# A hybrid encoder layer on one core: the queues planned with later landings and longer issues for the scan's loads

## The chip, the cores and the metric

The kernel runs on one core of one Trainium2 chip. The time is that of one execution in device microseconds. Before the change three runs took 1288.22, 1292.00 and 1293.46 us; their median is 1292.0.

The core's engines each run a queue of their own in order: TensorE (PE) for matmuls, with PEld for its weight loads, VectorE (DVE), ScalarE (ACT), GpSimd (POOL), and SyncE (SP), which here issues every transfer. An instruction that waits holds up all that stands behind it in its queue.

## The reference

One layer of an encoder, sequence 2048, width 1024, all in fp32. A normalised input is projected once; the columns go to two groups of heads, whose results are joined, projected and added to the input.

```python
h = rms_norm(x, norm_w)
dn_q, dn_k, dn_v, dn_z, dn_beta, dn_decay, sw_q, sw_k, sw_v, sw_z = split(h @ w_in)
# A: 4 heads of 128, gated delta rule, forward and backward
q, k, v = silu(depthwise_conv5(concat(dn_q, dn_k, dn_v)))
q, k = l2_norm(q) * 128 ** -0.5, l2_norm(k)
fwd = delta_rule(q, k, v, g[:, :, 0], beta[:, :, 0])
bwd = flip(delta_rule(flip(q, k, v, g[:, :, 1], beta[:, :, 1])))
dn = rms_norm(fwd + bwd, out_norm_w) * silu(dn_z)
# B: 8 query heads of 64, 2 key heads, |i - j| <= 128, QK-norm, rotary, a sink logit per head
sw = windowed_attention(sw_q, sw_k, sw_v) * silu(sw_z)
x = x + concat(dn, sw) @ w_out

def delta_rule(q, k, v, g, beta):       # per chunk: t_inv = (I + m)^-1, then a scan over chunks
    v_new = u - w @ state
    o = (q * exp(g)) @ state + a @ v_new
    state = state * exp(g_last) + k_dec.T @ v_new
```

## The kernel before

**Stages.** `phase_a` makes the projections in two halves of 1024 rows. A fp32 product is made of three matmuls, with weights and input split into a high and a low part (`wh`/`wl`, `xhi`/`xlo`): `pf_c` and `pf_z` are projections with the features on the partitions, `pq` with the rows there. Attention for 128 rows at a time runs between them (`s`, `pt`, `po`). The convolution is made on VectorE in `acc`. Results go to DRAM: `kq_d` and `v_d` per delta head, `zdn` and `zsw_d` for the gates, `mix_sw` for the attention.

`phase_b` does the delta rule, chunks of 128 rows, two directions (`d`), heads 0 to 3. `pre_front(h)` loads k and q (`kq`, 512 rows each, two buffers), transposes them (`tr`), makes their products (`gh`) and the decayed matrices `ma`, which go to DRAM as `m_d`. `pre_back(h)` inverts: it loads the diagonal 32x32 blocks of `m_d` into `L0` and `L` and unit matrices into `X` (from `eye`), solves them in 31 steps on VectorE (`tm`, `X`, lines L704 and L708), writes `X` to DRAM as `x_d`, reads it back in blocks as `xc` (two directions by four groups of chunks), spreads these to `ut` and `tt`, and joins the blocks with matmuls `pza`, `pra`, `pzb`, `prb`. `scan(h)` then goes over 16 steps in both directions; each step loads `at` (64 KB of `m_d`) and, from the second on, `kqc` (128 KB of `kq_d`), each with three buffers per direction:

```python
at = rp.tile([P, P], F32, tag=f"at{d}", name=f"at{nm}", bufs=3)
dma(at, m_d[d, c, : 2 * P * P].rearrange("(i a j) -> i a j", a=2, j=P)[:, 1])
kqc = rp.tile([P, 2, P], F32, tag=f"kqc{d}", name=f"kqc{nm}", bufs=3)
dma(kqc, kq_d[h][:, :, sc])
T.matmul(pk, kqc[:, 0], st[d], start=True, stop=True)
```

The matmul above (L785) is the first of a step, `po<-S,kqc` (L795) the last reader of `kqc`, and `po<-y,at` (L811) that of `at`. `post` norms and gates a head (`tro`, `zt`) and stores it in `mix_dn`.

The output projection has two halves. That of the attention (`pcs`, weights `woss`, inputs `mls`) has no part in the chain of the delta heads; its 16 chunks are put between the scans, and the partial sums go to DRAM as `part`. That of the delta heads (`pcd`, weights `wosd`, inputs `mld`, and `xrd` and `x2d`, the partial sum and the residual) ends the program.

**What sets the order.** The code does not. `set_order` takes all instructions and plans the five queues together: it gives each a price (`cost` for the time on its engine, SP's issues included; `landing` for the time from a transfer's issue until its reader may start), walks forward and backward with the prices, tries 120 random variations with a fixed seed, and keeps the plan that ends first by its own prices. The plan is then fixed as the order of each queue. So a price changes no instruction, only the order.

Of the kernel before, what the change touches and what calls it, by code (L numbers as in the profile page):

```python
# [892 lines left out]
def set_order(tc):  # L893
# [9 lines left out]
    n = len(insts)  # L903
    tiles = {x.name: x for x in tc.tiles}

    def aps(l):
        return [a.bass_ap for a in l if hasattr(a, "bass_ap")]

    def size(a):
        r = 1  # L910
        for _, c in list(a.ap)[1:]:
            r *= c
        return r
# [107 lines left out]
    def cost(i, eng):  # L1021
        o = aps(i.outs)
        m, ins = size(o[0]), aps(i.ins)
        if eng == "SP":
            dims = max(sum(c > 1 for _, c in list(a.ap)[1:]) for a in (o[0], ins[0]))
            return 450 if dims < 2 else 560
        off = 115 * (o[0].ap[0][0] > 0 and o[0].offset // o[0].ap[0][0] % P > 0)
        if eng == "PE":
            if i.is_transpose:
                return 110  # L1030
            if "float32r" in str(i.ins[0].dtype):
                return max(111, 0.4435 * m + 5.5)
            return 2 * max(m * 0.855, 112)
        scalars = sum(size(a) == 1 for a in ins)
        if eng == "Activation":
            psum = any("PSUM" in str(tiles[a.tensor.name].space) for a in ins if a.tensor.name in tiles)
            return 82 - 42 * psum + 0.865 * m + 92 * (scalars > 0) + 92 * (len(o) > 1) + off
        m = max([m] + [size(a) for a in ins])
        if eng == "DVE":
            if i.opcode == "Reciprocal":  # L1040
                return 62 + 6.2 * m
            if i.opcode == "TensorScalarPtr" and len(ins) - scalars < 2:
                return 58 + 0.6 * m
            return 68 + 1.04 * m + 60 * (scalars > 0) + 10 * (i.opcode == "ISA") + off
        if i.opcode == "TensorTensor":
            return 350 + 160 * m if m <= 16 else 140 + 2.165 * m
        return 250 + 0.8 * m + 0.4 * off

    def landing(i):
        o, a = aps(i.outs)[0], aps(i.ins)[0]  # L1050
        n = o.ap[0][1] * size(o) * 4
        if o.tensor.name in tiles and "DRAM" in str(tiles[o.tensor.name].space):
            return 1800 + n / (450 if sum(c > 1 for _, c in o.ap) < 3 else 190)
        run = min([c for t, c in list(a.ap) + list(o.ap) if t == 1] or [1])
        return 1900 + n / 190 + 1000 * any(t == 0 for t, _ in a.ap) + 1200 * (run < 64)

    total = len(succ)
    dur = [cost(i, e) for i, e in insts] + [0] * (total - n)
    eng = [e for _, e in insts] + [None] * (total - n)
    move, late = [0.0] * total, [0.0] * total  # L1060
    nxt, prv = [[] for _ in range(total)], [[] for _ in range(total)]
    for k in range(total):
        if eng[k] == "SP":
            a = aps(insts[k][0].outs)[0]
            move[k] = a.ap[0][1] * size(a) * 4 / 300
            late[k] = landing(insts[k][0])
        lag = LAG[eng[k]] + late[k] if k < n else 0
        if eng[k] == "Activation" and len(aps(insts[k][0].outs)) > 1:
            lag += 90
        for s in succ[k]:  # L1070
            if eng[s] == eng[k] != "SP":
                nxt[k].append((s, SAME[eng[k]] * ((k, s) in wrote)))
            else:
                nxt[k].append((s, lag))
        for s in started[k] if k < n else ():
            nxt[k].append((s, None))
        for s, d in nxt[k]:
            prv[s].append((k, d))
# [182 lines left out]
```

## Time and profile before

| | |
|---|---|
| median of three runs | 1292.0 us |
| execution that was profiled | 1291.88 us |
| its span, first to last instruction | 1290.1 us |
| mean granted TensorE clock | 0.989 |
| TensorE busy | 1220.2 us (95%) |
| VectorE busy | 939.1 us (73%) |
| ScalarE, GpSimd busy | 700.8 us, 486.3 us |
| moved by DMA | 218.01 MB, mean 169 GB/s |

Busy times are unions over the span. In rows of the timeline the first number is the start after the span's start in us, the second the duration; SPq rows are the issues of transfers, whose duration includes a wait at the head of the queue. In square brackets stands how long the engine was idle ahead of the row, and what ended that.

### The profile page before, as it was taken

How to read it: one execution, taken by the hardware profiler on the slowest of the kernel's cores; microseconds unless marked ns; L12 is line 12 of the kernel's file. 1: busy time of each engine (PE TensorE's matmuls, PEld its weight loads, DVE VectorE, ACT ScalarE, POOL GpSimd, SP SyncE). 2: the span in 40 equal slices, each digit the busy share in tenths (PEclk: the TensorE clock that was granted, in tenths of full speed). 3: DMA queues.
4: the chain of work that ended last, by engine and by line, in shares of the span. 5: the costliest groups of instructions: out<-in, count | busy, mean ns of one | idle time of the engine just before them, and what ended most of it. 6: DMA issues, size and time to landing. Idle time of an engine off the chain costs nothing.

```text
span 1290.1 us, 22274 instructions
## 1 busy us (share of the span) xinstructions
PE 1220.2 (95%) x7034; PEld 1043.6 (81%) x7034; DVE 939.1 (73%) x2346; ACT 700.8 (54%) x2057; POOL 486.3 (38%) x606
## 2 busy tenths in 40 slices
PE   4999999999999999999999999699999999998998
PEld 4998878888899987787778877587788788986776
DVE  4312477777888778799997878789779888766443
ACT  5322254435677777877755455476566655555211
POOL 1330214104667677886312313512422320213333
PEclk9999999999999999999999999799999999999999
DMA  8453244325542344421247567878868765378897
GB/s 259 129 144 104 82 145 146 119 86 173 162 123 81 113 117 135 137 88 67 74 146 265 177 175 240 221 190 256 236 158 255 248 160 159 100 230 272 250 309 227
DMA packets 238519, 218.01 MB, mean 169 GB/s; under 512 B 50624, under 2 KB 189632, under 8 KB 238400
## 3 DMA queue, kind: packets, MB, share of 16 engines
q1 hardware_dynamic: 238400, 216.58, 55.4%
q8 instruction: 56, 0.92, 0.3%
q14 instruction: 63, 0.52, 0.1%
HBM read 143.05 MB, written 73.47 MB: 168 GB/s over the span
## 4 chain that ended last, share of the span: by engine, by line
PE 75%; DMA 10%; DVE 6%; ACT 4%; issue 2%; SPq 2%; POOL 1%; DVEq 0%; ACTq 0%; POOLq 0%
PE pf_c L188 6%; PE pf_c L189 6%; PE pf_c L190 6%; PE pf_z L189 3%; PE pf_z L188 3%; PE pf_z L190 3%; PE pt L362 3%; PE pq_q L199 2%; PE pq_q L200 2%; PE pq_q L201 2%; PE pcs L566 2%; PE pcd L567 2%; PE gh L656 2%; PE pcs L567 2%; PE pk L793 2%
## 5 line engine op out<-in xcount | busy, mean ns | idle before, releaser
L239 DVE SCALAR_TENSOR_TENSOR acc<-pf_c,cw,acc 128x512 f32<-128x512 f32 (+2 forms) x192 | 140.6, 745 | 28.1 <-ACT acc L235 22.7
L188 PE MATMUL pf_c<-xhi,wh_c 128*128 128x512 f32 x384 | 150.8, 401 | 1.1 <-DVE acc L239 0.9
L189 PE MATMUL pf_c<-xlo,wh_c 128*128 128x512 f32 x384 | 151.6, 401 | 0.0
L190 PE MATMUL pf_c<-xhi,wl_c 128*128 128x512 f32 x384 | 149.5, 400 | 0.0
L357 POOL TENSOR_SCALAR pr<-pr,st 128x384 f32<-128x384 f32 (+1 forms) x128 | 84.6, 681 | 62.9 <-DVE st L355 32.4
L189 PE MATMUL pf_z<-xlo,wh_z 128*128 128x512 f32 x256 | 100.3, 404 | 0.0
L188 PE MATMUL pf_z<-xhi,wh_z 128*128 128x512 f32 x256 | 99.9, 404 | 0.0
L190 PE MATMUL pf_z<-xhi,wl_z 128*128 128x512 f32 x256 | 99.7, 402 | 0.0
L348 ACT ACTIVATE pr<-pr,st 128x384 f32<-128x384 f32 (+1 forms) x128 | 76.1, 596 | 21.3 <-DVE st L347 18.2
L188 PEld LDWEIGHTS pf_c<-xhi,wh_c 128*128 128x128 f32 x384 | 72.3, 188 | 16.8 <-DVE acc L239 1.6
L189 PEld LDWEIGHTS pf_c<-xlo,wh_c 128*128 128x128 f32 x384 | 72.2, 188 | 14.7
L190 PEld LDWEIGHTS pf_c<-xhi,wl_c 128*128 128x128 f32 x384 | 72.1, 188 | 14.5
L367 DVE TENSOR_TENSOR pl<-pt,ph 128x512 fp32r<-128x512 f32 x92 | 62.2, 685 | 23.2 <-ACT ph L366 22.4
L563 POOL TENSOR_TENSOR xrd<-xrd,x2d 128x512 f32<-128x512 f32 x32 | 42.3, 1324 | 95.9 <-DMA x2d<-x 35.3
L343 DVE CUSTOM_DVE_ANT_0 pr<-s,mask,sink 128x384 f32<-128x384 f32 (+1 forms) x128 | 73.4, 593 | 6.4 <-PE s L342 4.5
L362 PE MATMUL pt<-ident,pr 128*128 128x128 f32 x368 | 71.0, 275 | 2.3 <-POOL pr L357 1.0
L366 ACT ACTIVATE ph<-pt 128x512 fp32r<-128x512 f32 x92 | 53.7, 594 | 33.5 <-PE pt L362 27.1
L199 PE MATMUL pq_q<-wh_q,xhi 128*128 128x256 f32 x256 | 69.0, 289 | 0.8 <-ACT sgq L258 0.8
L200 PE MATMUL pq_q<-wh_q,xlo 128*128 128x256 f32 x256 | 69.5, 285 | 0.0
L201 PE MATMUL pq_q<-wl_q,xhi 128*128 128x256 f32 x256 | 68.2, 284 | 0.0
L798 ACT ACTIVATE yk<-pk,ck 128x128 f32<-128x128 f32 x120 | 44.1, 368 | 38.8 <-PE pk L793 38.1
L566 PE MATMUL pcs<-wohs,mhs 128*128 128x512 f32 x128 | 57.5, 449 | 6.0 <-ACT wohs L543 4.2
(251 smaller groups left out, 3775.1 us busy)
## 6 DMA issues: line engine op xcount, KB each, us to landing
m_d<-ma SPq DMA_DIRECT2D x32, 512.0 KB, 4.9
kqc<-kq_d SPq DMA_DIRECT2D x120, 128.0 KB, 3.3
ws_c<-wt SPq DMA_DIRECT2D x48, 256.0 KB, 3.4
xr<-x SPq DMA_DIRECT2D x16, 512.0 KB, 5.9
ws_z<-wt SPq DMA_DIRECT2D x32, 256.0 KB, 3.7
kq<-kq_d SPq DMA_DIRECT2D x16, 512.0 KB, 5.5
at<-m_d SPq DMA_DIRECT2D x128, 64.0 KB, 2.9
part<-xrs SPq DMA_DIRECT2D x32, 256.0 KB, 3.2
```

Source lines behind the costliest of these rows:

```text
L188: T.matmul(ps, hi[:, k, cs], xhi[b][:, k], start=(k == 0), stop=False)
L189: T.matmul(ps, hi[:, k, cs], xlo[b][:, k], start=False, stop=False)
L190: T.matmul(ps, lo[:, k, cs], xhi[b][:, k], start=False, stop=(k == KC - 1))
L199: T.matmul(ps[:, :n], xh, hi[:, k, :n], start=(k == 0), stop=False)
L200: T.matmul(ps[:, :n], xl, hi[:, k, :n], start=False, stop=False)
L201: T.matmul(ps[:, :n], xh, lo[:, k, :n], start=False, stop=(k == KC - 1))
L239: V.scalar_tensor_tensor(av, ps[:, lo:], cw[:, i, k : k + 1], av, ALU.mult, ALU.add)
L343: V.tensor_tensor_reduce(pr[j][:, :n], ps[:, :n], mask[:, lo * P : hi * P], 1.0, sink[:, hh : hh + 1], ALU.add, ALU.max, accum_out=mx[:, j ...
L348: A.activation(pr[j][:, :n], pr[j][:, :n], AF.Exp, bias=nm[:, j : j + 1], accum_out=den[:, j : j + 1])
L357: G.tensor_scalar(pr[j][:, :n], pr[j][:, :n], den[:, j : j + 1], 1.0, ALU.mult, ALU.mult)
L362: T.transpose(pt[:, j], pr[j][:, (kb - lo) * P : (kb - lo + 1) * P], ident)
L566: T.matmul(ps, mh[:, k], wh[:, k, ns], start=(k == 0), stop=False)
```

## The change

Two prices of the planner change. SP's issue of the scan's two loads, `at` and `kqc`, is priced at 630 ns instead of 450 and 560. The landing of every transfer is priced 700 ns later: stores to DRAM 2500 ns plus size instead of 1800, loads 2600 instead of 1900.

```diff
         if eng == "SP":
             dims = max(sum(c > 1 for _, c in list(a.ap)[1:]) for a in (o[0], ins[0]))
-            return 450 if dims < 2 else 560
+            return 630 if o[0].tensor.name.startswith(("at", "kqc")) else 450 if dims < 2 else 560
...
-            return 1800 + n / (450 if sum(c > 1 for _, c in o.ap) < 3 else 190)
+            return 2500 + n / (450 if sum(c > 1 for _, c in o.ap) < 3 else 190)
         run = min([c for t, c in list(a.ap) + list(o.ap) if t == 1] or [1])
-        return 1900 + n / 190 + 1000 * any(t == 0 for t, _ in a.ap) + 1200 * (run < 64)
+        return 2600 + n / 190 + 1000 * any(t == 0 for t, _ in a.ap) + 1200 * (run < 64)
```

The queues of all five engines are drawn anew by it. Three places on SP follow. In the names the head comes first, then for `at`, `kqc` the direction and the step, for `xc` the direction and the group of chunks; the last number is a buffer's.

SP at the end of the projections, where the first solve begins and `kq1_1`, the first rows of head 1, are loaded; `ws_z14` are weights of the last projections. Before:

```order
L698 DMA L0_9506<-m_d0_8595 64x32x32
L699 DMA X0_9507<-eye32 128x1024
L697 DMA L00_9505<-m_d0_8595 64x32x32
L178 DMA ws_z14_1_4_8283<-wt 128x2x256
L619 DMA kq1_1_9767<-kq_d1_88 128x2x512
```

and now:

```order
L698 DMA L0_9506<-m_d0_8595 64x32x32
L697 DMA L00_9505<-m_d0_8595 64x32x32
L699 DMA X0_9507<-eye32 128x1024
L619 DMA kq1_1_9767<-kq_d1_88 128x2x512
L178 DMA ws_z14_1_4_8283<-wt 128x2x256
```

The second half of the blocks has gone ahead of the unit matrices, and `kq1_1` ahead of the weight load.

SP where the solve of head 0 ends, from its store `x_d0` to the read-backs `xc0`; `dc2` are decay rows of head 2. Before:

```order
L709 DMA x_d0_8596<-X0_9507 128x1024
L670 DMA m_d1_9765<-ma1_0_0_9934 128x4x256
L629 DMA dc2_1_0_11099<-gr_d_5040 128x4x128
L757 DMA xc0_0_0_9578<-x_d0_8596 128x4x32
L629 DMA dc2_1_1_11103<-gr_d_5040 128x4x128
L781 DMA at0_0_0_10090<-m_d0_8595 128x128
L757 DMA xc0_1_0_9584<-x_d0_8596 128x4x32
L784 DMA kqc0_0_1_10122<-kq_d0_87 128x2x128
L699 DMA X1_10835<-eye32 128x1024
L757 DMA xc0_0_3_9592<-x_d0_8596 128x4x32
```

and now:

```order
L784 DMA kqc0_0_1_10122<-kq_d0_87 128x2x128
L709 DMA x_d0_8596<-X0_9507 128x1024
L781 DMA at0_1_0_10105<-m_d0_8595 128x128
L784 DMA kqc0_1_1_10143<-kq_d0_87 128x2x128
L542 DMA woss_1_0_8889<-wout 128x512
L781 DMA at0_0_1_10120<-m_d0_8595 128x128
L784 DMA kqc0_0_2_10164<-kq_d0_87 128x2x128
L542 DMA woss_1_1_8893<-wout 128x512
L784 DMA kqc0_1_2_10185<-kq_d0_87 128x2x128
L757 DMA xc0_0_0_9578<-x_d0_8596 128x4x32
L781 DMA at0_1_1_10141<-m_d0_8595 128x128
L757 DMA xc0_1_0_9584<-x_d0_8596 128x4x32
```

Between the store and the read-backs now stand the scan's first loads and two slices of `woss`; `m_d1`, `dc2` and `X1` have gone behind the first read-backs. `kqc0_0_1` ahead of the store needs memory of the projections, and waits for the last but one of their matmuls, `pf_z15_1_1`. The third slice, `woss_2_0`, stands 29 places behind `x_d0` before and 16 now. The load `L01` of head 1 follows 40 places behind `x_d0` before, behind `at0_0_3`, which waits for the matmul `po0_0_0`; now it follows 43 places behind, behind `kqc0_1_4`, which waits for `po0_1_1`. For head 3, `kq3_1` and the two loads of L ahead of it stood behind the last read-back of head 1, `xc1_1_2`, and now stand ahead of it.

SP in the middle of the last scan, two steps in both directions; `xrd`, `x2d` and `mld` are inputs of the last output projection, `wosd` its weights. Before:

```order
L784 DMA kqc3_0_8_14084<-kq_d3_90 128x2x128
L781 DMA at3_0_8_14082<-m_d3_12421 128x128
L553 DMA mld7_14543<-mix_dn3_100 128x3x128
L784 DMA kqc3_1_8_14105<-kq_d3_90 128x2x128
L781 DMA at3_1_8_14103<-m_d3_12421 128x128
L562 DMA x2d7_0_14552<-x 128x512
L561 DMA xrd7_1_14571<-part7_8537 128x512
L784 DMA kqc3_0_9_14126<-kq_d3_90 128x2x128
L781 DMA at3_0_9_14124<-m_d3_12421 128x128
L562 DMA x2d7_1_14572<-x 128x512
L784 DMA kqc3_1_9_14147<-kq_d3_90 128x2x128
```

and now:

```order
L784 DMA kqc3_0_8_14084<-kq_d3_90 128x2x128
L573 DMA part15_8545<-xrs15_0_9473 128x512
L781 DMA at3_0_8_14082<-m_d3_12421 128x128
L784 DMA kqc3_1_8_14105<-kq_d3_90 128x2x128
L852 DMA zt2_2_13323<-zdn2_97 128x512
L781 DMA at3_1_8_14103<-m_d3_12421 128x128
L784 DMA kqc3_0_9_14126<-kq_d3_90 128x2x128
L784 DMA kqc2_1_15_13430<-kq_d2_89 128x2x128
L781 DMA at3_0_9_14124<-m_d3_12421 128x128
L784 DMA kqc3_1_9_14147<-kq_d3_90 128x2x128
L781 DMA at2_0_15_13412<-m_d2_11093 128x128
L542 DMA wosd_0_0_14511<-wout 128x512
```

`mld`, `x2d` and `xrd` have left this stretch; the last loads of head 2's scan have come into it. From `kqc3_0_5` to `kqc3_0_12` are 50 places before and 44 now.

## The prediction

> **What bounds the kernel now.** I read the page's head first, then the busy time by stage, then the waits of TensorE at its long gaps, then the issue queue of SP at those places. The page:
>
> ```profile
> span 1290.1 us, 22274 instructions
> PE 1220.2 (95%) x7034; PEld 1043.6 (81%) x7034; DVE 939.1 (73%) x2346; ACT 700.8 (54%) x2057; POOL 486.3 (38%) x606
> ```
>
> TensorE is busy for 1220.2 of 1290.1 us. No matmul is added or removed, so an order of the queues can win only from the other 69.9 us and from time at a lowered clock. Where these lie, by stage (columns: busy time of each engine with its count, granted clock, DMA share, GB/s):
>
> ```profile
> 26.00:750.00 724.00, 716.49 (x4011) 612.07 (x4010) 528.84 (x1224) 411.07 (x1002) 322.63 (x476) 1.00 0.41 129
> 750.00:850.00 100.00, 83.99 (x426) 69.06 (x425) 78.13 (x187) 50.42 (x179) 31.20 (x23) 0.91 0.78 219
> 850.00:1120.00 270.00, 257.34 (x1729) 228.40 (x1728) 227.35 (x680) 163.13 (x611) 78.88 (x57) 0.99 0.69 198
> 1120.00:1200.00 80.00, 70.21 (x477) 61.55 (x476) 53.04 (x163) 45.16 (x182) 15.72 (x11) 0.98 0.75 228
> 1200.00:1291.00 91.00, 82.77 (x359) 64.33 (x357) 37.37 (x71) 15.89 (x52) 33.38 (x25) 0.99 0.83 266
> ```
>
> The projections and attention (26 to 750) leave 7.5 us idle in 724: nothing to win there. The change of stage (750 to 850) leaves 16.0 idle and loses 9 more at a clock of 0.91; the three scans and solves after it leave 12.7; the last scan and its surroundings 9.8; the output projection 8.2, the end included. So some 45 us lie in reach at most, and the question is which of them hang on a load that was planned too late.
>
> **The prices against the rows.** Median landings, then the issue of the scan's two loads:
>
> ```profile
> kqc<-kq_d SPq DMA_DIRECT2D x120, 128.0 KB, 3.3
> at<-m_d SPq DMA_DIRECT2D x128, 64.0 KB, 2.9
> ws_c<-wt SPq DMA_DIRECT2D x48, 256.0 KB, 3.4
> q_d<-sgq SPq DMA_DIRECT2D x32, 128.0 KB, 1.8
> 1130.52 0.60 SPq L781 DMA_DIRECT2D at<-m_d  x1
> 1131.22 0.52 SPq L784 DMA_DIRECT2D kqc<-kq_d  x1
> ```
>
> The planner's old price for a kqc load is 1900 + 131072/190 = 2590 ns, the new one 3290: the row says 3.3. For at it is 2245, then 2945: the row says 2.9. For ws_c it is 3280, then 3980, and for the store q_d 2091, then 2791: there the old price is the nearer. An at issue at 1130.52 is followed 0.70 later by kqc: against 450 and 560 before, 630 for both is right. So the plan becomes truer in the scans and over-cautious in the projections, where there is little idle time to lose.
>
> **The change part by part.** No instruction is added or removed; all five queues are drawn anew, and I cost the places where TensorE waits.
>
> First, the kq load of head 1 and the start of the first solve:
>
> ```profile
> 746.72 1.55 SPq L699 DMA_DIRECT2D X<-eye  x1
> 748.33 0.60 SPq L697 DMA_DIRECT2D L<-m_d  x1
> 749.04 2.93 SPq L178 DMA_DIRECT2D ws_z<-wt  x1
> 752.06 0.55 SPq L619 DMA_DIRECT2D kq<-kq_d  x1
> 757.68 1.09 PE L636 MATMUL tr<-ident,kq 128*128 128x128 f32 x4 [3.09 <-DMA kq<-kq_d]
> 750.00:775.00 25.00, 21.91 (x101) 17.64 (x100) 18.56 (x50) 10.49 (x43) 3.32 (x3) 0.93 0.68 196
> ```
>
> The kq load stands behind a weight load that holds SP for 2.93; TensorE waits 3.09, and the clock of 0.93 over these 25 us costs 1.75 more. In the change kq1 stands ahead of that weight load, about 3.0 sooner, and its reader stands behind some more projection matmuls. I take the stall as gone: 4.8 on TensorE (0 if the load slips for another reason). The Trainium skill, TensorE: Matmul & The Clock Gate, Part 1: The HAM clock gate, has the clock halve after an idle window of about 3.4 us. Here 3.09 idle was enough, and the loss fits one such window at half speed; by the rule taken strictly this stall costs no clock and 1.75 less would be won; the row decides.
>
> But what follows is not TensorE's alone. The solve of head 0 runs on VectorE and its result X leaves at 799.89:
>
> ```profile
> 799.89 0.33 SPq L709 DMA_DIRECT2D x_d<-X  x1
> 803.79 0.62 PE L190 MATMUL pf_z<-xhi,wl_z 128*128 128x512 f32 x2
> 805.50 0.42 SPq L757 DMA_DIRECT2D xc<-x_d  x1
> 811.68 0.31 DVE L758 STREAM_TRANSPOSE xt<-xc 128x128 f32<-128x128 f32 x1 [1.19 <-DMA xc<-x_d]
> 813.68 2.05 PE L720 MATMUL pza<-ut,wm 128*128 128x128 f32 x8 [5.60 <-DVE ut L761]
> 821.28 0.38 SPq L542 DMA_DIRECT2D woss<-wout  x1
> 827.77 0.51 PE L566 MATMUL pcs<-wohs,mhs 128*128 128x512 f32 x1 [4.18 <-ACT wohs L543]
> 833.27 0.49 PE L793 MATMUL pk<-vs,tt 128*128 128x128 f32 x2 [0.24 <-ACT tt L748]
> ```
>
> In the change the store of X stands behind kqc0_0_1, which waits for one of the last projection matmuls (they end at 804.4 here). With the 4.8 won above these end at about 799.6, just when X is ready, so the store leaves at about 800: no gain, no loss. The second read-back, xc0_1_0, is then ten places behind it: ten issues at 0.6 give 806, against 805.50 now. But now it lands only at 811.7, 6.2 after its issue, behind a 512 KB store, two 256 KB loads of decay rows and the load of eye; in the change those stand behind it, and kqc, at and two woss loads ahead. Between 2.9 (at) and 6.2 I take 3.8, nearer the small loads that are its neighbours: it lands at 809.8, and the first inversion matmul starts 2.0 later (813.68 less 811.68), at 811.8 instead of 813.7: 1.9 sooner (0.4 later to 2.8 sooner). The third slice of woss, at 821.28 now, stands 16 places behind x_d, at about 810; its stall of 4.18 goes. Together the first scan step, now at 833.27, comes 6 sooner (0 to 9).
>
> Second, what takes that back: the load of L for head 1, which starts the next solve.
>
> ```profile
> 836.53 0.61 SPq L697 DMA_DIRECT2D L<-m_d  x1
> 843.02 0.39 PE L795 MATMUL po<-S,kqc 128*128 128x128 f32 x2
> 912.79 0.41 SPq L709 DMA_DIRECT2D x_d<-X  x1
> ```
>
> In the change it stands behind kqc0_1_4, which waits for po0_1_1, the matmul at 843.02 here. Six sooner that is 837.0: no earlier than now. The solve then runs its 76 us (836.53 to 912.79) on VectorE, so the second x_d leaves near 912.8 again, and TensorE waits there for the time that it came ahead. It keeps what it has worked off meanwhile: between 850 and 1120 it is busy 257.34 of 270, VectorE 227.35, so TensorE is nearer its own limit than the solve's. I let 4 of the 6 be lost (0 to 6). Net of the first two heads: 2.
>
> Third, kq of head 3, the same pattern as the first:
>
> ```profile
> 935.15 2.28 SPq L698 DMA_DIRECT2D L<-m_d  x1
> 937.47 2.47 SPq L619 DMA_DIRECT2D kq<-kq_d  x1
> 944.21 0.66 PE L636 MATMUL tr<-ident,kq 128*128 128x128 f32 x4 [2.84 <-DMA kq<-kq_d]
> 925.00:950.00 25.00, 20.30 (x128) 17.67 (x128) 18.66 (x37) 15.64 (x63) 14.38 (x10) 0.93 0.87 223
> ```
>
> Here the stall is 2.84 and the clock costs 1.75. The change puts L and kq ahead of the last xc read-back, which waits for a buffer. I take 3 of the 4.6 (0 to 4.6).
>
> Fourth, the last scan. Between its fifth and twelfth step, 1131.2 to 1161, the queue issued (x count, KB, landing):
>
> ```profile
> kqc<-kq_d SPq DMA_DIRECT2D x17, 128.0 KB, 3.5
> at<-m_d SPq DMA_DIRECT2D x18, 64.0 KB, 3.2
> xrd<-part SPq DMA_DIRECT2D x4, 256.0 KB, 3.9
> x2d<-x SPq DMA_DIRECT2D x3, 256.0 KB, 3.9
> 1160.93 0.53 SPq L784 DMA_DIRECT2D kqc<-kq_d  x1
> PE pk L785 <- DMA kqc<-kq_d: 2.7, 4, 1.0
> ```
>
> From kqc3_0_5 (the row at 1131.22 above) to kqc3_0_12 (1160.93) are 50 places in 29.7 us: SP issues without a pause, 0.594 each, and each step's first matmul takes its kqc as it lands. The change has 44 places there; xrd, x2d and mld for the output projection stand behind. Six places are 3.6 us; I take 3.5 (0 if buffers of three steps, not places, set the pace). Their cover: the output projection begins only with the last scan's own result, and the wosd weights stand earlier than before. If that fails, xrd is late there next.
>
> Last, the projections: an order drawn anew over 724 us with prices that are too late there. I charge 1 (0 to 3).
>
> The sum: 2 + 3 + 3.5 - 1 = 7.5. The execution profiled took 1291.88, 1.8 more than its span, and lies on the median of 1292.0; 1291.9 - 7.5 = 1284.4.
>
> **Rivals.** That the solves set everything: the head start is all given back (6 instead of 4), kq3 wins 1 instead of 3, and the scan's buffers allow 1.5 of 3.5; 7.5 - 2 - 2 - 2 = 1.5, some 1290. For it speaks the load of L1, which comes no earlier; against it TensorE's 95%.
>
> Slower: the store of X waits at the head of SP's queue. If the first stall stays, the projections end at 804.4, and x_d0 leaves 4.8 later than now; the first scan step is then not sooner but 3 later, and L1, behind po0_1_1 at 843 and over, comes 6.5 to 9 later than 836.53. With the charge of 1 and the 3.5 of the last scan that is 5 to 8 slower, some 1299. It decides from the point where the last projection matmul ends after X is ready. For it: the order itself, and X is ready at 799.89 against 804.4. Against it: kq1 is ahead of what delayed it.
>
> That nothing changes is excluded by the queues, which differ from the first rows on.
>
> **How the numbers follow.** About 0.5%, 6.5 us, is what a measurement here can tell from no change. My sum lies just past it: faster 0.48. The solves decide: 0.32, nearly all of it within 0.5%. Slower: 0.20. The range takes in all stalls gone, that is both takings-back at zero (7.5 + 4 + 1 = 12.5, to 1279, and some 6 of the other idle time at 850 to 1120) down to 1273, and up to the slow rival at 1299.
>
> **What would show it.** Right: no wait of tr for kq near 755; x_d0 issued by 801; the first scan step by 829; kq3 without a wait over 2; the last scan's step 5 to 12 in about 26 us. Wrong: x_d0 at 804, L1 after 840, new TensorE gaps over 2 us in 100 to 750, or waits of the output projection for xrd.

## The result: slower by 1.2%, most of it lost before the first solve

The changed kernel takes 1305.97 us (median of six runs, 1304.99 to 1309.85), the kernel before beside it 1291.58 (1288.22 to 1293.46): ratio 1.0121, interval 1.0101 to 1.0140. The execution profiled is the longest of its six, 1309.85. One run of the experiments, 4203 us in e12, whose other nine took 1291 to 1298, is not in its ratio. The head of the changed kernel's page and its busy time by stage (columns as in the prediction):

```profile
span 1307.8 us, 22293 instructions
PE 1225.7 (94%) x7034; PEld 1042.2 (80%) x7034; DVE 953.7 (73%) x2346; ACT 702.8 (54%) x2057; POOL 481.4 (37%) x606
...
26.00:750.00 724.00, 710.79 (x3955) 604.46 (x3955) 531.51 (x1212) 404.29 (x976) 314.45 (x474) 1.00 0.40 127
750.00:850.00 100.00, 87.87 (x435) 70.53 (x433) 81.98 (x176) 50.34 (x175) 36.55 (x27) 0.95 0.78 218
850.00:1120.00 270.00, 251.05 (x1663) 218.04 (x1663) 229.05 (x681) 164.27 (x623) 77.36 (x57) 1.00 0.70 199
1120.00:1200.00 80.00, 72.43 (x539) 66.30 (x538) 54.61 (x174) 50.84 (x196) 10.25 (x7) 0.98 0.67 203
1200.00:1308.00 108.00, 95.20 (x416) 75.68 (x414) 43.26 (x85) 17.91 (x58) 37.86 (x29) 0.97 0.80 259
```

Read the count in the first row. By 750 us TensorE has done 3955 matmuls of this stretch, before 4011; 56 at 716.49 / 4011 = 0.18 us are some 10 us, an estimate, since matmuls differ in size. In that stretch the prediction had charged 1. The idle time there grew from 7.5 to 13.2, which is 5.7 of it; 3.4 more are time at a lowered clock near 425 (below).

The places that the prediction named, from SP's and TensorE's timelines of the changed kernel:

```profile
761.20 0.62 SPq L698 DMA_DIRECT2D L<-m_d  x1
772.80 0.63 PE L636 MATMUL tr<-ident,kq 128*128 128x128 f32 x4 [1.18 <-DMA kq<-kq_d]
814.01 0.55 SPq L709 DMA_DIRECT2D x_d<-X  x1
843.13 0.39 PE L793 MATMUL pk<-vs,tt 128*128 128x128 f32 x2
852.72 0.61 SPq L697 DMA_DIRECT2D L<-m_d  x1
926.21 0.38 SPq L709 DMA_DIRECT2D x_d<-X  x1
958.36 0.66 PE L636 MATMUL tr<-ident,kq 128*128 128x128 f32 x4 [0.41 <-DMA kq<-kq_d]
1145.35 1.18 SPq L784 DMA_DIRECT2D kqc<-kq_d  x2
1172.82 0.52 SPq L784 DMA_DIRECT2D kqc<-kq_d  x1
```

The kernel before loads these first blocks of L at 746.06:

```profile
746.06 0.62 SPq L698 DMA_DIRECT2D L<-m_d  x1
```

So the first solve starts 15.1 us later, its result leaves 14.1 later (814.01 against 799.89), the next L 16.2, the next result 13.4. Up to the second result these places are shifted by what was lost ahead of 750. At the end the profiled execution is 18.0 longer than that of before (1309.85 less 1291.88).

### The profile page after: what moved, and what is told of

It is laid out like the page before. It is cut to its first block, busy times and chain, and to the rows that moved or that the text cites. A ratio compares the mean times of both kernels' runs of the same rounds, so it can differ in the third digit from the quotient of the medians.

```text
span 1307.8 us, 22293 instructions
## 1 busy us (share of the span) xinstructions
PE 1225.7 (94%) x7034; PEld 1042.2 (80%) x7034; DVE 953.7 (73%) x2346; ACT 702.8 (54%) x2057; POOL 481.4 (37%) x606
## 4 chain that ended last, share of the span: by engine, by line
PE 74%; DVE 8%; ACT 5%; DMA 5%; issue 4%; POOL 2%; SPq 1%; POOLq 0%; ACTq 0%; DVEq 0%
PE pf_c L188 6%; PE pf_c L189 6%; PE pf_c L190 6%; PE pf_z L188 4%; PE pf_z L190 4%; PE pf_z L189 4%; PE pt L362 2%; PE po L795 2%; PE po L811 2%; PE pk L802 2%; PE gh L656 2%; PE pk L785 2%; PE pk L793 2%; PE pq_q L199 2%; PE pcs L566 2%
## 5 line engine op out<-in xcount | busy, mean ns | idle before, releaser
L189 PE MATMUL pf_c<-xlo,wh_c 128*128 128x512 f32 x384 | 148.3, 397 | 0.0
L672 POOL TENSOR_TENSOR wm<-ma,ma 128x512 f32<-128x512 f32 x16 | 22.8, 1424 | 105.5 <-DVE ma L665 28.1
```

The costliest lines, as they stand in the source:

```text
L189: T.matmul(ps, hi[:, k, cs], xlo[b][:, k], start=False, stop=False)
```

## The experiments

Each ratio is to the kernel before on the same chip, with its 95% interval; one per cent is 12.9 us. The table gathers them all with three readings of their profiles: TensorE's idle time in 26 to 750, and the matmuls done by stage. The profile of e5 is that of the shortest of its seven runs (1299.15, their median is 1308.45).

| kernel | ratio (interval) | idle, 26-750 | matmuls 26-750 | 750-850 | 850-1120 |
|---|---|---|---|---|---|
| before | 1 | 7.5 | 4011 | 426 | 1729 |
| changed | 1.0121 (1.0101 to 1.0140) | 13.2 | 3955 | 435 | 1663 |
| e1 issue price alone | 0.9966 (0.9947 to 0.9985) | 7.7 | 4007 | 510 | 1678 |
| e2 landings alone | 1.0033 (1.0011 to 1.0056) | 12.9 | 3964 | 452 | 1705 |
| e3 before, other seed | 0.9989 (0.9965 to 1.0012) | 10.0 | 3968 | 481 | 1726 |
| e4 changed, other seed | 1.0074 (1.0048 to 1.0100) | 14.6 | 3950 | 472 | 1670 |
| e5 changed front | 1.0095 (1.0065 to 1.0125) | 13.4 | 3963 | 425 | 1724 |
| e6 changed middle | 1.0008 (0.9989 to 1.0027) | 9.1 | 4006 | 459 | 1681 |
| e7 changed tail | 1.0031 (1.0015 to 1.0048) | 8.3 | 4007 | 421 | 1718 |
| e8 changed middle and tail | 1.0008 (0.9992 to 1.0025) | 8.5 | 4007 | 484 | 1678 |
| e9 changed, no table load | 1.0084 (1.0050 to 1.0118) | 11.3 | 3979 | 450 | 1665 |
| e10 changed to 343, then before | 1.0106 (1.0068 to 1.0144) | 14.5 | 3952 | 397 | 1693 |
| e11 changed from 340 to 736 | 1.0081 (1.0057 to 1.0105) | 11.8 | 3972 | 429 | 1680 |
| e12 late landings in the projections | 1.0000 (0.9973 to 1.0026) | 11.3 | 3978 | 481 | 1710 |
| e13 late q, kv round trip | 1.0033 (1.0018 to 1.0047) | 12.8 | 3954 | 427 | 1715 |
| e14 three parts | 0.9979 (0.9952 to 1.0005) | 8.6 | 4008 | 469 | 1704 |
| e15 late landings after the projections | 1.0017 (1.0001 to 1.0033) | 6.4 | 4007 | 407 | 1761 |
| e16 before, no table load | 0.9986 (0.9970 to 1.0001) | 6.9 | 4014 | 428 | 1721 |
| e17 early q, kv round trip | 0.9971 (0.9956 to 0.9986) | 8.6 | 4001 | 492 | 1691 |

**Which price, or only the draw?** e1 keeps the new issue price alone, e2 the new landings alone, e3 and e4 change the seed of the trials.

```diff
-            return 2500 + n / ...    # e1: 1800 and 1900 again
-            return 630 if o[0].tensor.name.startswith(("at", "kqc")) else ...    # e2: out
-    rnd = random.Random(1)
+    rnd = random.Random(2)           # e3 on before, e4 on the changed kernel
```

> The issue price alone (630 ns for at and kqc on SP), the landings as before. Theory A, the later landings cost the time, in the projections and attention: this one loses nothing there and wins part of the last scan, so 1287 to 1291 us, with no more idle TensorE in 26 to 750 than the 7.5 us of before. Theory B, any new draw of the queues moves the time by some ten microseconds in a chance direction: 1285 to 1306, and where it loses differs from the changed kernel. Theory C, the issue price is what costs (the scan's loads are planned slower, so the scan is stretched): 1300 or more, lost after 850.

> The later landings alone (700 ns more for every load and store), the issue prices as before. Theory A: nearly all of the loss, 1302 to 1309 us, of which 8 to 13 in the stretch from 26 to 750, where TensorE gets through fewer matmuls by 750 than before. Theory B: anywhere in 1285 to 1306. Theory C: about 1290.

> The kernel before with another seed of the planner's random trials: the prices are the old ones, the queues are drawn anew. Theory A: within 5 us of 1291.6, since the prices are the same. Theory B: as far from 1291.6 as the change is, some 10 us either way.

> The changed kernel with another seed of the planner's random trials. Theory A: 1300 to 1311 us, lost again in 26 to 750. Theory B: anywhere in 1285 to 1311, and as likely below 1296 as above it.

The issue price alone makes the kernel faster by 0.34%, which rules theory C out; the landings alone cost 0.33%. One other seed moves before by less than its interval and the changed kernel by about 0.5%, and it stays slower. As far as one seed for each can tell, a pure lottery (B) does not explain the sign, but a part of the size is a draw. Theory A has the sign and the stretch, but not the size: it had the landings alone at 1302 to 1309, and 1291.6 times their ratio is 1296. The two prices do not add up: 0.33 less 0.34 would be zero, not 1.21.

**Where?** The change moves no instruction in or out, so a queue may follow one plan up to a point of time and the other from there on. e5, e6 and e7 take the changed order in one of three parts alone (to some 745 us, from there to some 1110, from there to the end), e8 in the last two. `fixed_queues` holds the five queues, written out; the planner's search, which stood ahead of these lines, is left out.

```diff
-    end, begin, queue = best
+    queue, end = fixed_queues(), 0    # e5: changed to 745 us, then before
```

> The queues of the changed kernel up to about 745 us (every instruction that its plan starts before then), after that those of the kernel before, for all that is left. Theory A, the loss is made in the projections and carried to the end: ratio to before 1.008 to 1.012 (10 to 15 us). Theory D, the first solve on VectorE swallows it (TensorE waits there anyway), and the loss is made after 750: 0.998 to 1.004.

> The queues of before up to about 740 us, those of the changed kernel from there to about 1110 us, then those of before again. Theory A: a gain, 0.994 to 0.998, since the stalls of kq and woss that the prediction counted go. Theory D: 1.004 to 1.009, lost at the second head's inversion, between 860 and 960.

> The queues of before up to about 1110 us, then those of the changed kernel: last scan and output projection. Theory A: a gain of 2 to 3 us from the scan, 0.997 to 0.999. Theory D: a loss of 2 to 4 us, since the output projection's weights and rows come late there, 1.001 to 1.004.

> The queues of before up to about 740 us, then those of the changed kernel to the end. Theory A: the gains that were predicted come out unspoilt, 0.992 to 0.998 (1281 to 1289 us). Theory D: most of the loss is still there, 1.006 to 1.012.

The front alone, with the rest in the order of before, costs 0.95%, 12.3 us (8.4 to 16.2); the middle 0.08% (1.0 us); the tail 0.31% (4.0 us, 1.9 to 6.2). The sum is 1.34 against 1.21 (1.01 to 1.40). Theory A holds on the front, and theory D's verdict on that (the first solve swallows the loss) is refuted: e5 does no more in 750 to 850 than before (425 matmuls, 426), and it entered that stretch late: its first load of L starts at 755.73, before at 746.06, and its second result leaves at 921.04, before at 912.79. On the middle (e6, and with it e8) neither was right, and on the tail D was. Behind the changed middle the tail's loss does not show (e8: 0.08 for both, where e6 and e7 give 0.39), but the intervals are too wide to tell these apart. With the front of before, the middle shows what the prediction's own steps were worth. e8, timelines:

```profile
801.49 0.56 SPq L709 DMA_DIRECT2D x_d<-X  x1
829.80 0.39 PE L793 MATMUL pk<-vs,tt 128*128 128x128 f32 x2
839.27 0.61 SPq L697 DMA_DIRECT2D L<-m_d  x1
913.55 0.38 SPq L709 DMA_DIRECT2D x_d<-X  x1
```

and its stages:

```profile
750.00:850.00 100.00, 87.27 (x484) 72.12 (x482) 81.34 (x192) 53.81 (x189) 33.67 (x24) 0.97 0.81 221
850.00:1120.00 270.00, 252.77 (x1678) 220.12 (x1677) 227.31 (x679) 161.27 (x611) 76.83 (x56) 1.00 0.68 195
```

From 750 to 850 it does 58 matmuls more (484 against 426), and the first scan step is 3.5 us sooner (829.80, before 833.27). From 850 to 1120 it does 51 fewer (1678 against 1729): nearly all is given back. The second result leaves at 913.55, before at 912.79.

**What in the front.** Two places are told apart first. Near 425 TensorE has its longest gap after the start. ScalarE's, VectorE's and TensorE's rows of the changed kernel there:

```profile
424.85 1.28 ACT L348 ACT_TABLE_LOAD   x1 [0.91 <-DVE st L347]
426.15 0.61 ACT L348 ACTIVATE pr<-pr,st 128x384 f32<-128x384 f32 x1
428.24 0.21 ACT L352 ACTIVATE st<-st 128x4 f32<-128x4 f32 x1
428.48 0.16 DVE L353 SCALAR_TENSOR_TENSOR st<-st 128x4 f32<-128x4 f32 x1 [2.64 <-ACT st L352]
428.67 0.42 DVE L376 TENSOR_TENSOR ot<-po,ot 64x256 f32<-64x256 f32 x1
429.23 0.76 PE L369 MATMUL po<-ph,v 128*128 128x512 f32 x1 [3.54 <-DVE ot L376]
```

Read it backwards. TensorE waits for the `po` buffer that L376 frees; L376 is ready but stands behind L353 in VectorE's queue, which waits for an exponential, which stands on ScalarE behind the load of an activation table. One logarithm (L464) makes two such loads, 1.28 us each, which no price of the planner knows. The Trainium skill, ScalarE: Activation LUTs, What ACT_TABLE_LOAD costs, gives about 1283 ns for the load, which the trace has, and about 1380 ns more for a drain. For that the kernel before has no room on either side: its second load starts 0.02 after the instruction ahead has ended, and the next instruction starts 0.01 after the load.

```profile
421.28 0.38 ACT L258 ACTIVATE sgq<-pq_q 128x256 f32<-128x256 f32 x1
421.68 1.28 ACT L348 ACT_TABLE_LOAD   x1
422.97 0.62 ACT L348 ACTIVATE pr<-pr,st 128x384 f32<-128x384 f32 x1
```

e9 and e16 put a copy in place of the logarithm, which leaves the logarithm out of the result and the two loads with it (e9 on the changed kernel with its queues unchanged, e16 on before):

```diff
-    A.activation(m, w, AF.Ln)
+    A.activation(m, w, AF.Copy)
```

> The queues of the changed kernel, unchanged, with the one logarithm on ScalarE (of the decay's softplus) made a copy: it leaves the logarithm out, and with it the two loads of an activation table around it (1.28 us each, at 420.8 and 424.9). Theory T: TensorE's 3.54 us gap at 425.7 and the half clock behind it (6.8 us at half speed, 3.4 lost) come from these two loads, which the planner's prices do not know; without them 5 to 7 us come back: ratio to before 1.005 to 1.009. Rival: that gap would come from another wait (the sums of attention on VectorE and ScalarE are late in any case): 1.010 to 1.013, as the changed kernel.

> The kernel before with its logarithm made a copy, which leaves the logarithm out and the two table loads with it. Theory T: here the loads fall where other work covers them: 0.998 to 1.001. Rival: they cost their 2.6 us or more in any order: 0.995 to 0.998.

The stretch behind the gap, changed kernel and then e9:

```profile
427.00:436.00 9.00, 6.77 (x28) 6.39 (x29) 5.63 (x18) 4.84 (x13) 6.40 (x12) 0.62 0.26 83
```
```profile
427.00:436.00 9.00, 9.00 (x67) 8.42 (x68) 7.23 (x23) 6.75 (x18) 7.31 (x12) 1.00 0.32 99
```

Without the loads the gap shrinks from 3.54 to 0.73 us and the clock stays at 1.00 instead of 0.62 (9 x 0.38 = 3.4 lost). That is 2.8 + 3.4 = 6.2 us, the 5 to 7 of theory T, at that place. At the end of the run 1.0084 lies where T put it, but its interval does not exclude the rival. In the kernel before, the same loads cost 0.14%, and the interval reaches zero.

The second: e10 follows the changed order to 343 us only, e11 from 340 to 736 only.

> The changed kernel's queues up to about 343 us, then those of before. In it the score matmuls of attention chunk 1 stand behind 877 of the 960 gate and convolution matmuls of the first half (before: 552), but chunk 3 and all later ones stand as before. Theory E1, the late start of attention makes the loss, since a chunk cannot follow the one ahead in less than some 26 us: 1.006 to 1.010, TensorE waiting between 340 and 470 until the chunks have caught up. Theory E2, the loss is made where the chunks then stand close together without filler, and in the second half: 1.000 to 1.004 (the 3 us of the first 75).

> The queues of before up to about 340 us, those of the changed kernel from there to about 736 us, those of before for the rest. Chunks 1 and 2 stand early, chunk 3 behind all filler and 722 matmuls of the next projection (before: 582). Theory E1: 0.999 to 1.003. Theory E2: 1.005 to 1.009, with 5 us lost near 425 and 4 near 600.

Both are slow, so each theory missed the other half. What they share is work put off. From 240 to 340 us, all engines and then the first score matmuls (L341) alone; before, changed:

```profile
240.00:340.00 100.00, 100.00 (x477) 82.24 (x476) 77.53 (x154) 50.34 (x107) 30.90 (x44) 1.00 0.42 130
240.00:340.00 100.00, 4.98 (x14) 2.65 (x14) 1.00 0.42 130
```
```profile
240.00:340.00 100.00, 100.00 (x461) 81.53 (x460) 74.10 (x136) 43.32 (x81) 18.00 (x32) 1.00 0.43 141
240.00:340.00 100.00, 2.84 (x9) 1.43 (x8) 1.00 0.43 141
```

TensorE is full in both. But in the changed order it spends the filler (gate and convolution projections) and does 9 score matmuls instead of 14; ScalarE does 43 us of work instead of 50, GpSimd 18 instead of 31. Of the score matmuls (eight a chunk) the changed kernel has done 16 by 340 us, before 24. The other runs fall in with that: e1, e3, e15 and e17 have done 24, e13 20, and e2, e4 and e12, which price all landings of the projections late, 16. The work that was put off comes back when the filler is gone. e10 asks for it at once, and TensorE stands; here 340 to 375 us, before and e10:

```profile
340.00:375.00 35.00, 35.00 (x249) 33.02 (x248) 28.33 (x77) 24.87 (x64) 27.41 (x42) 1.00 0.50 154
```
```profile
340.00:375.00 35.00, 29.02 (x168) 24.01 (x168) 24.20 (x76) 22.98 (x61) 21.66 (x33) 0.90 0.26 79
```

That is 6.0 us idle and 35 x 0.10 = 3.5 of clock. e11 puts attention off from 340 on and pays near 425 and 600: TensorE is idle for 3.6 us in 375 to 440 and 5.4 in 570 to 670, before for 1.1 and 2.2.

**Which transfers.** e12 and e15 give the later landings to one side each; e13 to four transfers alone, the round trip of q and kv through memory; e17 prices that round trip earlier. All four keep the new issue price; other landings are the old ones.

```diff
+            late[k] = landing(insts[k][0]) + 700 * (k < 6884)     # e12; e15: k >= 6884
...
+            if ends_at.startswith(("kv_d", "q_d", "kv", "ql")):
+                late[k] += 700                                     # e13; e17: late[k] -= 450
```

> The new issue price, and the 700 ns for the transfers of the projections and attention alone; those of the scans and solves keep the old landing. Theory A: the projections' own transfers, priced too late, order the front badly: 1.006 to 1.012. Rival: the front is bad because the later part, planned longer, sets other priorities in it: 0.996 to 1.003.

> The old landings and the new issue price, with 700 ns more for four transfers alone: the stores of the projected q and kv and their loads by attention, a round trip that becomes 1.4 us longer. In its queues chunk 1 stands behind 854 filler matmuls (before 552, changed 877), chunk 2 behind 912 (887, 955), chunk 3 behind 650 of the next projection (582, 722). Theory A2, this round trip is the road: TensorE 5 to 9 us behind before at 736 and ratio to the issue price alone 1.004 to 1.008, so 1.000 to 1.005 to before. Rival, the weights' loads and the gates' stores are the road: as the issue price alone, 0.994 to 0.999.

> The new issue price, and the 700 ns for the transfers of the scans, solves and output projection alone. Theory A: the front is left alone (TensorE within 2 us of before at 736), 0.996 to 1.002. Rival, the later landings cost in the later part too: 1.004 to 1.008.

> The old landings and the new issue price, with the same four transfers (stores of q and kv, loads by attention) 450 ns earlier instead of 700 later: 1.64 and 2.8 us for q, near the medians of 1.8 and 3.3 that the kernel before shows. In its queues chunk 1 stands behind 805 filler matmuls (before 552), but chunk 2 behind 882 and chunk 3 behind 576 of the next projection, both a little earlier than before (887, 582). Theory A2, what counts is that chunks 2 and 3 come early enough: 0.993 to 0.998, the front within 2 us of before. Rival, a late chunk 1 costs by itself: 1.002 to 1.006.

e13 against e1 is a change of these four prices alone: 1.0033 / 0.9966, 0.67% more, and 53 matmuls fewer by 750 (3954, 4007). e17 turns them the other way and keeps the front (4001) and the gain (0.9971). 240 to 340 us again, e13 and e17:

```profile
240.00:340.00 100.00, 99.46 (x462) 81.11 (x461) 73.61 (x145) 45.81 (x91) 22.20 (x34) 1.00 0.39 120
240.00:340.00 100.00, 4.30 (x12) 2.26 (x12) 1.00 0.39 120
```
```profile
240.00:340.00 100.00, 100.00 (x481) 82.22 (x480) 77.80 (x167) 51.33 (x109) 28.04 (x47) 1.00 0.38 122
240.00:340.00 100.00, 6.11 (x17) 3.18 (x17) 1.00 0.38 122
```

In e17 chunk 1 is late too, but it is made up for: the ninth, 17th and 25th score matmuls, with which chunks 1, 2 and 3 begin if they run in order, start near 294, 322 and 350 us (before 233, 321, 337; changed 316, 344, 372), and ScalarE has its 51 us. A late chunk 1 by itself costs nothing. A later price of the round trip is therefore one road to the loss; an earlier one loses nothing. Whether the price is true does not decide it. For q the old prices are the nearer (2.09 us for the store and 3.28 for the load; new 2.79 and 3.98), for kv the new ones (2.79 and 3.29; old 2.09 and 2.59). The store q_d took 1.8, and the others:

```profile
ql<-q_d SPq DMA_DIRECT2D x16, 256.0 KB, 3.3
kv_d<-sgkv SPq DMA_DIRECT2D x16, 128.0 KB, 2.7
kv<-kv_d SPq DMA_DIRECT2D x16, 128.0 KB, 3.0
```

e17 prices kv earlier still, and keeps its front.

e15 leaves the front alone (4007 matmuls), as theory A had it, and 1.0017 lies in its range. Against e1, which has the issue price too, it is 0.51% slower, and e12 0.34%; both late prices together, the changed kernel, are 1.56% slower (each ratio has an interval of 0.2 to 0.3 either way). So the two sides do not add up either, and later landings behind the projections won nothing, although for at and kqc they are the truer ones.

e12 is the exception to the loss in the front. All the projections' transfers are late in it, 16 score matmuls by 340 as in the changed kernel, and it is behind at 750 (3978); it ends level with before. In 750 to 850 it does 481 matmuls, as does e3. Nor is a front that is as late as that of e5 always as dear: the first load of L starts at 757.64 in e2 and 755.14 in e13 (e5 755.73, before 746.06), and both end 0.33% behind, e5 0.95%. So a loss in the front can be made good in part where the order behind it allows it, and the 12.3 us are its price with the order of before. What it is in those orders that makes it good stays open.

**Do the gains add up?** e14 joins the front of before, the middle of e12 and the tail of e3.

> Queues in three parts: before to about 725 us, then those of the kernel with late prices in the projections alone (e12) to about 1025, then those of before with another seed (e3). By the profiles the middle part gained 11 us on before and the last part held its own. Theory F, parts add up: 0.990 to 0.995. Rival, the solves of the next heads on VectorE take the head start back: 0.997 to 1.003.

0.9979: the head start of the middle (469 against 426) is more than half lost again by 1120 (1704 against 1729). The rival was nearer. The versions that are faster than before by more than their interval are e1 and e17, by 0.3%.

## Why the prediction was wrong

The step that failed is the last term, "the projections: I charge 1 (0 to 3)", with its reason, "little idle time to lose". Idle time bounds what can be won, not what can be lost. e5 measures the term: 12.3 us (8.4 to 16.2) in place of 1. What the runs showed in place of that reason is work of attention put off behind filler, with TensorE full, and paid for later in idle time and clock. The forecast was 7.5 us faster, the result is 14.4 slower (1305.97 less 1291.58). The front is some 11 of these 22; the middle and the tail, promised 5 and 3.5 faster and measured 1.0 and 4.0 slower, are 6 and 7.5, and the three overlap within their intervals.

*kq of head 1.* Right in direction: a wait of 1.18 in place of 3.09, not zero.

*x_d, xc, woss, the first scan step.* With the front of before (e8) x_d leaves at 801.49, about the 800 foreseen, and the first scan step comes 3.5 sooner, not 6. In the changed kernel these steps are 14.1 and 9.9 us late, all of it older than they are.

*Given back.* "4 of 6" was too little. L comes at 839.27 in e8, 2.7 later than before, and the second result 0.8 later: everything is given back. That is the rival "the solves set everything", and for the middle it was the better forecast: e6 is 1.0 us slower (1.4 faster to 3.5 slower), where the terms 2 + 3 promised 5 faster.

*kq of head 3.* The wait is 0.41 in place of 2.84, as foreseen ("without a wait over 2"); the middle as a whole kept none of it.

*The last scan.* From the second of the two issues at 1145.35 to 1172.82 are 26.9 us, before 29.7: 2.8 won of the 3.5 foreseen. But "their cover", the output projection, failed. The changed tail alone (e7) ends 4.0 us later. TensorE's longest waits there from 1120 on, and then the two longest of before in its output projection (from 1190 on):

```profile
PE pcd L567 <- DVE mld L555: 4.9, 4, 2.1
PE po L811 <- ACT y L800: 2.0, 1, 2.0
PE pcd L566 <- DVE zt L853: 1.7, 1, 1.7
PE pcd L566 <- ACT mhd L554: 1.4, 1, 1.4
```
```profile
PE pcd L566 <- ACT mhd L554: 2.6, 3, 1.8
PE pcd L567 <- DVE mld L555: 2.6, 4, 1.3
```

And its clock:

```profile
1120.00:1200.00 80.00, 71.78 (x495) 64.01 (x495) 53.16 (x170) 45.97 (x182) 15.26 (x11) 0.96 0.74 228
1200.00:1296.00 96.00, 83.76 (x364) 66.32 (x362) 38.01 (x70) 16.38 (x55) 32.98 (x25) 0.97 0.80 262
```

Against 0.98 and 0.99 before, that is 80 x 0.02 + 96 x 0.02 = 3.5 us of clock. No wait names xrd, of which the prediction had warned. What is waited for longer than before is the low part of the split input (`mld`, 4.9 against 2.6) and the gate `zt`, both on VectorE, and in the scan `y` on ScalarE (2.0 against 1.1); `mhd` is waited for less. Why they are late stays open.

*The slow rival.* The time came out on its side, and 7 us beyond its 1299, but not by its mechanism. X takes 52.8 us from its load of L to its store (761.20 to 814.01), before 53.8. VectorE's last step on X ends at 813.32, so the store was held up at SP's head for 0.7 us, not 4.8. The rival's own terms, 6.5 to 9 and 1 less 3.5, give 4 to 6.5 slower, not the 5 to 8 that it says. Nor do the stages add up to "some 45 us" in reach: idle time alone is 46.7, and with the 9 of clock 55.7.

*The prices.* That the landings become "over-cautious in the projections" was read from q_d and ws_c. The rows of kv say the contrary. That 630 is right for the issue of at and kqc is borne out by e1.

"New TensorE gaps over 2 us in 100 to 750" was named as what would show the prediction wrong; the one of 3.54 at 425 is it.

## What to carry to other kernels

When a change redraws the order of a stretch in which TensorE is 99% busy, charge it with what a bad order can cost there, not with the idle time it shows: filler spent early leaves TensorE full and lets ScalarE's, VectorE's and GpSimd's work pile up, and here that was paid later. Change prices one at a time and measure each: the issue price of at and kqc was wrong by its rows, and putting it right was worth 0.34%; their landings were wrong by their rows too, and the truer ones (e15, with all others behind the projections) won nothing. A head start at a chain that another engine paces was in two runs (e8, e14) largely given back by the next solve.

## What was not expected of the hardware

Two short waits close together were enough to halve TensorE's clock. In e13 between 587 and 600, a matmul ahead of them, the waits, and the same matmul behind them:

```profile
587.35 0.39 PE L188 MATMUL pf_c<-xhi,wh_c 128*128 128x512 f32 x1
594.54 0.44 PE L362 MATMUL pt<-ident,pr 128*128 128x128 f32 x2 [1.97 <-POOL pr L357]
595.66 1.25 PE L362 MATMUL pt<-ident,pr 128*128 128x128 f32 x6 [0.69 <-POOL pr L357]
598.04 0.63 PE L188 MATMUL pf_c<-xhi,wh_c 128*128 128x512 f32 x1
```
```profile
590.00:600.00 10.00, 6.82 (x33) 5.05 (x32) 8.77 (x24) 7.53 (x20) 8.51 (x10) 0.81 0.01 4
```

From the start of this matmul to that of the next are 0.23 us ahead of the waits and 0.42 behind them. The ten microseconds hold 3.2 us of idle time in three pieces, none over 2.0, and their mean clock is 0.81. The Trainium skill, TensorE: Matmul & The Clock Gate, Part 1: The HAM clock gate, speaks of an idle window of about 3.4 us; the trace does not agree with that as the length of a gap.
